# Layer norm's order, panels of the second block on VectorE, and the first norms inside the query projection

## The chip, the core and the metric

The program runs on one core of one Trainium2 chip. The metric is the device time of one execution in microseconds (us): the median of three runs of the kernel before is 1155.9 us (1153.77 to 1156.81).

The engines are named as the profile names them: PE (TensorE matmul), PEld (its weight loads), DVE (VectorE), ACT (ScalarE), POOL (GpSimd) and SP (SyncE, which here only issues the weight DMAs).

## What is computed

The reference is a two-block transformer forward in float32, with 256 tokens, width 1024 and one batch. The first block's parts, in order:

```python
# layer 0: x = x + conformer_conv(rms_norm(x))
u = h @ w_pw1 + b_pw1                          # 1024 -> 2048
a, gate = jnp.split(u, 2, axis=-1)
u = a * jax.nn.sigmoid(gate)                   # the gated linear unit ("glu")
u = depthwise_conv31(u, w_dw) + b_dw
u = jax.nn.silu(layer_norm(u, ln_g, ln_b))
x = x + u @ w_pw2 + b_pw2
# each layer then: x = x + memory_cross_attention(rms_norm(x), mem)
#                  x = x + swiglu(rms_norm(x))
# layer 1 has differential attention in place of the conv; rms_norm(x) at the end
```

The second block (`hybrid_layer`) projects the normed result once into queries, keys, values and gates, and attends in two families of eight heads each: a sliding window of 128 with sinks (the "w" heads), and a family with three branches (compressed, selected, window; the "n" heads). Its end is an output projection, and a feed-forward with a short causal conv.

```python
proj = rms_norm(h, attn_pre_norm) @ w_in        # q_n, k_c, v_c, k_s, v_s, k_w, v_w, g_n, q_w, k_sw, v_sw
ckv = compress(stack([rope(k_c), v_c]))         # windows of 32 tokens, stride 16 -> gelu MLP
o_swa = banded_attention(rope(q_w), rope(k_sw), v_sw, 128, sinks)
o_nsa = g0 * compressed + g1 * selected + g2 * banded(512)
h = h + rms_norm(concat(rms_norm(o_nsa), rms_norm(o_swa)) @ w_out)
```

## The kernel before

All projections are matmuls of a weight panel with activations. To keep float32 accuracy each operand is split into a rounded high part and the rest, and each product takes three matmuls: high by high, high by the activations' rest, and the panel's rest by high (line 409, in `gemm`). A panel is 128x1024 (512, 640 or 816 columns in some places). SP loads it into one of six stage buffers, ACT copies it to the high part `whi` (L276), and either DVE or POOL subtracts to get the low part `wlo` (L278). Which of the two does so is a cyclic string of letters for each weight in the table `LO`: `v` is DVE, `g` is POOL. The two parts stand in a ring of five buffers. Each time that `gemm` takes a panel (`consume`), it prepares panels up to `state["ahead"]`, five, beyond the one that it takes.

`gemm(K, xs, banks, evac, hooks)` runs K steps over the accumulator banks in PSUM (`acc`, six of them; two more are `aux`), calls the functions in `hooks` after the named step, and evacuates each bank at the end. The instructions of all engines are then ordered by a scheduler with priorities that follow the order in the source: a hook's place in the source decides roughly, not exactly, where its instructions stand in each engine's queue. Each engine's queue runs strictly in order.

RMS norms use the class `Stats`: squares on ACT, their sum `sacc` on POOL (L338; DVE for some), a fold of two halves `sfold` (L355), sums over partitions by PE with a column of ones (L361), a scale and offset on DVE (`ms`, L370), the power -1/2 on POOL (`rr`, L372), and where a row of factors is wanted over all partitions, `spread` on PE (L378). Layer norm after the conv has functions of its own: `ln_sum`, `ln_mean` (means by PE, subtraction, squares `lsq`, adds on DVE, L626) and `ln_rstd` (sums by PE, L632), which hang as hooks in the gemm of the memory's second value projection.

The places that the change touches:

- The glu after the first conv projection (L547 to L556), whose DVE operations scale the bank into an SBUF tile `t2`, then multiply.
- The layer norm's hooks (L622 to L645).
- The product `gfp` of two gain vectors (L959).
- The second block's start: `gemm(8, S0, BA, ...)` with the hook `norms` (L1000 on: two RMS norms chained, one through the other), then the first query projection `qw0`, whose hooks are `tables2` (spread and rotary tables `cR`, `sR`) and the evacuations `evA` of keys.
- The second block's attention, whose order is the list `ATT_SEQ`: `qw0`, `qw1`, `qn0`, `qn1` are query projections, `vt` values and gates, `xr` transposes of x, `ws` the window split (`winf`, `win`, on POOL and ACT, L1095 to L1097), `compk` and `compv` the compression MLPs, `a`, `b`, `c` with a number the scores, softmax and product with values of one head pair, `wo0` and `wo1` halves of the output projection. Scores are masked on DVE (L324), which also gives their maximum, and exponentiated on ACT (L1182 for the w heads).

## Time and profile before

| what | us |
|---|---|
| median of 3 runs | 1155.9 (1153.77 to 1156.81) |
| the profiled execution | 1154.35 |
| its span, first to last instruction | 1152.5 |
| PE busy | 1107.7 (96%) |
| DVE busy | 782.6 (68%) |
| ACT busy | 658.0 (57%) |
| POOL busy | 403.2 (35%) |

The profile is one execution. Times within it are counted from the span's start. PE's clock as granted by the chip is given as a share of full speed: 1.00 is 2.4 GHz, 0.50 is 1.2 GHz. A figure in square brackets behind a row is how long the engine sat idle before it, and what ended that idle time.

### The profile page before, as it was taken

The page shows a single profiled execution, that of the slowest core. Times are in us where ns is not written, and L with a number is a line of the kernel's source. Part 1 is how long each engine was busy: PE and PEld are TensorE (multiplying, and loading weights), DVE is VectorE, ACT ScalarE, POOL GpSimd, SP SyncE. Part 2 cuts the span into 40 slices and gives each one's busy share as a digit, 9 for nine tenths or more (in the row PEclk, how much of TensorE's full clock was granted, in tenths as well). Part 3 has the DMA queues.
Part 4 walks back from the last instruction along what each step waited for, and adds up shares of the span by engine and source line. Part 5 has one row for each costly group of instructions (what it writes and reads, how often), then busy time and mean ns, then how long its engine had stood idle before and what let it go on. Part 6 is the DMA issues. An engine that isn't in the chain of part 4 may idle for free.

```text
span 1152.5 us, 21545 instructions
## 1 busy us (share of the span) xinstructions
PE 1107.7 (96%) x8418; PEld 1048.2 (91%) x8418; DVE 782.6 (68%) x1432; ACT 658.0 (57%) x1165; POOL 403.2 (35%) x268
## 2 busy tenths in 40 slices
PE   7999989999999999999999999999988998999997
PEld 6898878999999999999899999999886678999986
DVE  6899867676676458766745655746678746887843
ACT  6555476665555345676756554536575745765632
POOL 5999947130000005731726443002662300112300
PEclk9999989999999999999999999999898998999999
DMA  7576535346545645544334654754563015464651
GB/s 248 191 256 208 195 110 182 124 140 211 189 150 200 215 152 166 196 133 129 128 127 158 197 182 144 253 173 137 181 200 130 19 56 182 152 205 161 226 191 37
DMA packets 59799, 191.13 MB, mean 166 GB/s; under 512 B 6752, under 2 KB 10080, under 8 KB 59696
## 3 DMA queue, kind: packets, MB, share of 16 engines
q1 hardware_dynamic: 58288, 187.31, 49.1%
q0 software_dynamic: 688, 1.90, 0.6%
q8 instruction: 66, 1.08, 0.4%
q10 hardware_dynamic: 720, 0.53, 0.1%
q14 instruction: 37, 0.30, 0.1%
HBM read 188.15 MB, written 1.05 MB: 164 GB/s over the span
## 4 chain that ended last, share of the span: by engine, by line
PE 46%; ACT 2%; DVE 2%; issue 2%; POOL 1%; POOLq 0%; DVEq 0%; ACTq 0%
PE acc L409 38%; PE acc L1125 1%; PE acc L1223 1%; ACT whi L276 1%; PE acc L696 1%; PE acc L730 0%; POOL sacc L338 0%; PE acc L1284 0%; PE acc L1288 0%; DVE wlo L278 0%; PE aux L1265 0%; PE acc L1377 0%; DVE memK1l L587 0%; PE acc L1285 0%; PE acc L1220 0%
## 5 line engine op out<-in xcount | busy, mean ns | idle before, releaser
L276 ACT ACTIVATE whi<-wf 128x1024 fp32r<-128x1024 f32 (+3 forms) x382 | 371.4, 987 | 301.4 <-PE acc L409 264.8
L278 DVE TENSOR_TENSOR wlo<-wf,whi 128x1024 fp32r<-128x1024 f32 (+2 forms) x261 | 327.8, 1264 | 183.7 <-ACT whi L276 178.3
L409 PE MATMUL acc<-s0h,whi 128*128 128x256 f32 x1192 | 338.5, 284 | 6.2 <-ACT whi L276 5.4
L409 PE MATMUL acc<-s0h,wlo 128*128 128x256 f32 x1192 | 335.5, 282 | 4.0 <-POOL wlo L278 3.6
L409 PE MATMUL acc<-s0l,whi 128*128 128x256 f32 x1192 | 335.7, 282 | 1.7 <-DVE s0l L437 1.7
L278 POOL TENSOR_TENSOR wlo<-wf,whi 128x1024 fp32r<-128x1024 f32 (+1 forms) x121 | 261.8, 2186 | 164.7 <-ACT whi L276 162.6
L409 PEld LDWEIGHTS acc<-s0h,whi 128*128 128x128 f32 x1192 | 226.7, 190 | 7.2 <-ACT whi L276 5.4
L409 PEld LDWEIGHTS acc<-s0h,wlo 128*128 128x128 f32 x1192 | 226.5, 190 | 5.7 <-POOL wlo L278 5.0
L409 PEld LDWEIGHTS acc<-s0l,whi 128*128 128x128 f32 x1192 | 226.9, 190 | 2.9 <-DVE s0l L437 2.1
L409 PE MATMUL acc<-s1h,whi 128*128 128x256 f32 x736 | 206.1, 281 | 0.7 <-ACT s1h L651 0.7
L409 PE MATMUL acc<-s1h,wlo 128*128 128x256 f32 x736 | 205.4, 279 | 0.7 <-DVE pad L665 0.4
L409 PE MATMUL acc<-s1l,whi 128*128 128x256 f32 x736 | 205.5, 280 | 0.0
L409 PEld LDWEIGHTS acc<-s1h,whi 128*128 128x128 f32 x736 | 138.3, 188 | 1.7 <-ACT s1h L651 1.4
L409 PEld LDWEIGHTS acc<-s1h,wlo 128*128 128x128 f32 x736 | 138.4, 188 | 1.1 <-DVE pad L665 0.7
L409 PEld LDWEIGHTS acc<-s1l,whi 128*128 128x128 f32 x736 | 138.6, 188 | 0.3 <-DVE pad L785 0.2
L409 PE MATMUL acc<-hh,whi 128*128 128x256 f32 x352 | 98.3, 279 | 0.0
L409 PE MATMUL acc<-hl,whi 128*128 128x256 f32 x352 | 98.3, 279 | 0.0
L409 PE MATMUL acc<-hh,wlo 128*128 128x256 f32 x352 | 98.3, 279 | 0.0
L338 POOL TENSOR_TENSOR sacc<-sq,sacc 128x512 f32<-128x512 f32 x21 | 33.3, 1588 | 124.0 <-ACT sq L337 123.7
L545 DVE SCALAR_TENSOR_TENSOR aux<-u,vecs,aux 128x256 f32<-128x256 f32 x174 | 68.6, 480 | 1.2 <-ACT aux L543 1.2
L409 PEld LDWEIGHTS acc<-hh,whi 128*128 128x128 f32 x352 | 66.2, 188 | 0.0
L409 PEld LDWEIGHTS acc<-hh,wlo 128*128 128x128 f32 x352 | 66.2, 188 | 0.0
(372 smaller groups left out, 1713.5 us busy)
## 6 DMA issues: line engine op xcount, KB each, us to landing
wf<-in_gu SPq DMA_DIRECT2D x120, 512.0 KB, 3.8
wf<-in_w_down SPq DMA_DIRECT2D x66, 512.0 KB, 4.3
wf<-in_mem_w_k SPq DMA_DIRECT2D x16, 512.0 KB, 4.0
wf<-in_mem_w_v SPq DMA_DIRECT2D x16, 512.0 KB, 3.5
wf<-in_mem_w_q SPq DMA_DIRECT2D x16, 512.0 KB, 3.5
wf<-in_mem_w_o SPq DMA_DIRECT2D x16, 512.0 KB, 3.7
wf<-in_w_pw SPq DMA_DIRECT2D x24, 256.0 KB, 3.0
wf<-in_gv SPq DMA_DIRECT2D x24, 256.0 KB, 2.6
```

What stands on the lines that cost most here:

```text
L276: p["ih"] = SC.activation(p["hi"][:, :W], p["f"][:, :W], AF.Copy)
L278: p["il"] = eng.tensor_tensor(p["lo"][:, :W], p["f"][:, :W], p["hi"][:, :W].bitcast(F32), op=OP.subtract)
L338: self.ins = self.eng.tensor_tensor(self.acc, sq, self.acc, op=OP.add)
L409: PE.matmul(o, l, r, start=(ki == 0 and n == 0 and q == 0), stop=(ki == K - 1 and q == 2), skip_group_check=True)
L545: V.scalar_tensor_tensor(cv[:, c] if k == TAPS - 1 else ai, src, w, ai, op0=OP.mult, op1=OP.add)
L696: PE.matmul(s[:, t * S:(t + 1) * S], l[:, c, t * 128:(t + 1) * 128], r[:, 2 * h + c], start=(t == 0 and c == 0 and n == 0), stop=(c == 1), ...
L1125: PE.matmul(ph[0:60, 0:256], win[:, a, 4 * g + j], w[:, j * 256:(j + 1) * 256], start=(g == 0 and j == 0 and w is p["hi"]), stop=(g == 3 a ...
L1223: PE.matmul(f, q1, kk[:, kv], start=True, stop=True, skip_group_check=True)
```

## The change

Seven edits are made together:

1. The glu multiplies in place in PSUM; the SBUF tile `t2` is gone.
2. `ln_mean` runs after step 3 (was 4), `ln_rstd` after step 6 (was 5). Of the three adds of squares on DVE two are left; the last group of squares goes through four more small matmuls instead. The spread factor is read from PSUM directly (`raw=True`), without ACT's copy.
3. `gfp` is issued after `st.ins`, which is a POOL instruction.
4. `norms` leaves the gemm `BA` (after its step 6) and goes into the gemm `qw0` (after its step 1); `tables2` and the key evacuations go from step 2 of `qw0` to its step 6.
5. In `LO`, `mq1` (second layer's memory query) goes from one panel in three on POOL to none; `T` (values, second block), `cmp` (compression) and `w` (output projection) go from one, two and one letter on POOL to none. Three panels of `mq1` and nine of the second block (one `T`, six `cmp`, two `w`) so move from POOL to DVE.
6. `ATT_SEQ` gets `few` after `qn0`: from there `ahead` is 1.
7. It also gets eight steps `p1` to `p5`: `pn` prepares panels up to n beyond those taken.

```diff
--- before.py
+++ after.py
@@ -62,10 +62,10 @@
 
 DIFF_SEQ = """q0 q1 a0 a1 V0 b0 a2 b1 a3 c0 q2 b2 c1 V1 b3 c2 a4 f0 c3 a5 q3 f1 b4 b5""".split()
 DIFF_END = {0: "a6 c4", 1: "a7 c5 b6", 2: "c6", (3, 1): "f2 b7", (4, 0): "c7", (5, 1): "f3"}
-ATT_SEQ = """... compk a4 qn0 compv c2 a5 b4 a6 comp2 c3 b5 c4 comp3 ... c7 a9 a10 b9 b10 a11 a12 c8 b11 c9 c10 a13 b12 c11 sw a14 a15 b13 c12 b14 wo0 c13 b15 wo1 c14 c15""".split()
+ATT_SEQ = """... compk a4 qn0 few compv c2 a5 b4 p1 a6 comp2 c3 b5 p2 c4 comp3 ... c7 a9 p1 a10 b9 p2 b10 a11 p3 a12 c8 b11 p4 c9 c10 a13 b12 p5 c11 sw a14 a15 b13 c12 b14 wo0 c13 b15 p4 wo1 c14 p4 c15""".split()
 LO = dict(pw1s="gv", pw1="g", mk="g", mv="g", pw2="gggvvvvv", mq="gggvvvvv", mo="vgv", gu0="v", gv0="v",
-          dn0="v", K="v", q="g", V="g", o="v", mq1="gvv", mo1="vgv", gu1="gv", gv1="v",
-          dn1="v", A="v", T="vvg", cmp="ggv", B="v", w="gv", W="v", gu2="v", gv2="vgv", dn2="v")
+          dn0="v", K="v", q="g", V="g", o="v", mq1="v", mo1="vgv", gu1="gv", gv1="v",
+          dn1="v", A="v", T="v", cmp="v", B="v", w="v", W="v", gu2="v", gv2="vgv", dn2="v")
 
 
 def _constants():
@@ -547,12 +547,10 @@
     def glu(c0):
         def f(j, ps):
             c = c0 + j
-            if 1:
-                t = poolC.tile([128, 2, S], F32, name="t2", tag="t2")
-                V.tensor_tensor(t, b2(ps), two(Rb[0]), op=OP.mult)
-                sg = poolC.tile([128, S], F32, name="sg", tag="sg")
-                SC.activation(sg, t[:, 1], AF.Sigmoid, bias=vc("b_pw1", 8 + c))
-                V.scalar_tensor_tensor(u[:, c, TAPS - 1:], t[:, 0], vc("b_pw1", c), sg, op0=OP.add, op1=OP.mult)
+            V.tensor_tensor(b2(ps), b2(ps), two(Rb[0]), op=OP.mult)
+            sg = poolC.tile([128, S], F32, name="sg", tag="sg")
+            SC.activation(sg, ps[:, S:2 * S], AF.Sigmoid, bias=vc("b_pw1", 8 + c))
+            V.scalar_tensor_tensor(u[:, c, TAPS - 1:], ps[:, 0:S], vc("b_pw1", c), sg, op0=OP.add, op1=OP.mult)
         return f
 
     def norm0():
@@ -622,15 +620,16 @@
             V.tensor_tensor(cp, cp, two(mu[:, :S]), op=OP.subtract)
             LN[j] = tmp.tile([128, 2, S], F32, name="lsq", tag="sq" if j else "sacc")
             SC.activation(LN[j], cp, AF.Square)
-            if j:
+            if 0 < j < 3:
                 V.tensor_tensor(LN[0], LN[0], LN[j], op=OP.add)
 
     def ln_rstd():
         ss = aux()
-        for i in range(2):
-            for t in range(2):
-                PE.matmul(ss[:, t:t + 1], LN[0][:, i, t * 128:(t + 1) * 128], ones[:, 0:1],
-                          start=(i + t == 0), stop=(i == 1), skip_group_check=True)
+        for j in (0, 3):
+            for i in range(2):
+                for t in range(2):
+                    PE.matmul(ss[:, t:t + 1], LN[j][:, i, t * 128:(t + 1) * 128], ones[:, 0:1],
+                              start=(j + i + t == 0), stop=(j == 3 and i == 1), skip_group_check=True)
         scr = small.tile([128, 2], F32, name="scr", tag="scr")
         SC.activation(scr[:, 0:1], LN[3][:, 0, 0:1], AF.Silu)
         LN["st"] = st = Stats(eps=1e-5)
@@ -639,10 +638,10 @@
     gemm(8, mT, FM8, mem_k(0))
     gemm(8, mT, TM4, mem_v(0))
     gemm(8, mT, FM8, mem_k(1))
-    gemm(8, mT, TM4, mem_v(1), hooks={2: [ln_sum], 4: [ln_mean], 5: [ln_rstd]})
+    gemm(8, mT, TM4, mem_v(1), hooks={2: [ln_sum], 3: [ln_mean], 6: [ln_rstd]})
     st = LN["st"]
     with tc.high_priority():
-        rs = spread(st.r)
+        rs = spread(st.r, raw=True)
         for s in (slice(0, 1), slice(1, 2), slice(2, 4), slice(4, 6), slice(6, 8)):
             cp = cv[:, s]
             V.tensor_tensor(cp, cp, rs[:, None, :].to_broadcast([128, s.stop - s.start, S]), op=OP.mult)
@@ -956,7 +955,8 @@
 
     sa, sb = Stats(), Stats()
     gfp = const.tile([128, 8], F32, name="gfp")
-    V.tensor_tensor(gfp, vecs[:, VOFF["g_final"][0]:VOFF["g_final"][0] + 8], vecs[:, VOFF["g_pre"][0]:VOFF["g_pre"][0] + 8], op=OP.mult)
+    with tc.issue_after(st.ins.ins):
+        V.tensor_tensor(gfp, vecs[:, VOFF["g_final"][0]:VOFF["g_final"][0] + 8], vecs[:, VOFF["g_pre"][0]:VOFF["g_pre"][0] + 8], op=OP.mult)
 
     def last(j, ps):
         xp = x[:, 2 * j:2 * j + 2]
@@ -1107,8 +1107,8 @@
 
     V.memset(kc2[64:128, :, :, S - 1:S], 0.0)
     pA = []
-    gemm(8, S0, BA, lambda j, ps: pA.append(ps), hooks={6: [norms]})
-    qw0_hooks = {2: [tables2] + [lambda j=j: evA(j, pA[j]) for j in range(3)]}
+    gemm(8, S0, BA, lambda j, ps: pA.append(ps))
+    qw0_hooks = {1: [norms], 6: [tables2] + [lambda j=j: evA(j, pA[j]) for j in range(3)]}
 
     kcmp = P1.tile([128, 2, 32], F32, name="kcmp")
     vcmp = P1.tile([32, 2, 64], F32, name="vcmp")
@@ -1306,7 +1306,9 @@
     steps = dict(xr=x2_rows, ws=window_split, vt=lambda: gemm(8, S0, [[("T", t, 0, 408)] for t in range(2)], evT),
                  qw0=lambda: q_(qw, 0, qw0_hooks), qw1=lambda: q_(qw, 1), qn0=lambda: q_(qn, 0), qn1=lambda: q_(qn, 1),
                  compk=lambda: comp(0), compv=lambda: comp(1), comp2=comp2, comp3=comp3, sw=sw.finish,
-                 wo0=lambda: wo1(0), wo1=lambda: wo1(1))
+                 wo0=lambda: wo1(0), wo1=lambda: wo1(1), few=lambda: state.update(ahead=1))
+
+    steps.update({f"p{n}": (lambda n=n: prep_to(state["use"] + n)) for n in range(1, 6)})
     for w in ATT_SEQ:
         if w in steps:
             steps[w]()
```

What the scheduler makes of it is seen in three places of the engines' orders. In them `wlo<-wf,whi` is a panel's subtraction, and the line numbers of the two kernels differ by up to two.

The first place is DVE around the second block's first norms: from the first norm's `ms` (L370) to the rotary tables (L1019, L1020). Before:

```order
L278 TENSOR_TENSOR wlo<-wf,whi 128x816
L370 TENSOR_SCALAR ms<-aux 128x2
L1008 TENSOR_TENSOR ms<-aux,rr 128x2
L278 TENSOR_TENSOR wlo<-wf,whi 128x816
L1009 TENSOR_TENSOR ms<-ms,rr 128x2
L1010 TENSOR_SCALAR ms<-ms 128x2
L1009 TENSOR_TENSOR ms<-ms,rr 128x2
L1010 TENSOR_SCALAR ms<-ms 128x2
L1019 TENSOR_TENSOR cR<-cst,aux 128x256
```

After:

```order
L278 TENSOR_TENSOR wlo<-wf,whi 128x816 x3
L370 TENSOR_SCALAR ms<-aux 128x2
L1008 TENSOR_TENSOR ms<-aux,rr 128x2
L1009 TENSOR_TENSOR ms<-ms,rr 128x2
L1010 TENSOR_SCALAR ms<-ms 128x2
L1009 TENSOR_TENSOR ms<-ms,rr 128x2
L1010 TENSOR_SCALAR ms<-ms 128x2
L278 TENSOR_TENSOR wlo<-wf,whi 128x816
L1019 TENSOR_TENSOR cR<-cst,aux 128x256
```

The panel subtraction that stood inside the chain of small operations now stands behind it. On PE the two sums of these norms (L361) stand 27 matmuls of `gemm` later than before, and the spread (L378) 24 later.

The second place is POOL from the key windows' DMAs to the first softmax operation of the n heads (L1253). `kc` are the shifted keys, `gp` is a gain row. Before:

```order
L1084 DMA kc_9653<-kcv 64x255
L278 TENSOR_TENSOR wlo<-wf,whi 128x1024 x3
L1095 TENSOR_TENSOR winf<-kc_9653,vecs 128x16x15 x2
L1097 TENSOR_TENSOR win<-winf,win 128x16x30
L1095 TENSOR_TENSOR winf<-kc_9653,vecs 128x16x15 x2
L1321 DMA gp_11139<-in_g_post 128x1024
L1097 TENSOR_TENSOR win<-winf,win 128x16x30
L278 TENSOR_TENSOR wlo<-wf,whi 128x1024 x5
L1253 TENSOR_SCALAR p<-p,dsm 128x128 x2
```

After:

```order
L1084 DMA kc_9646<-kcv 64x255
L1095 TENSOR_TENSOR winf<-kc_9646,vecs 128x16x15 x2
L1097 TENSOR_TENSOR win<-winf,win 128x16x30
L1095 TENSOR_TENSOR winf<-kc_9646,vecs 128x16x15 x2
L1323 DMA gp_11132<-in_g_post 128x1024
L1097 TENSOR_TENSOR win<-winf,win 128x16x30
L1253 TENSOR_SCALAR p<-p,dsm 128x128 x2
```

All eight panels have left; the window sums follow the DMAs at once.

The third place is DVE at the last masked scores (L324) ahead of the first n-head queries. Before:

```order
L278 TENSOR_TENSOR wlo<-wf,whi 128x1024
L324 ISA acc,mx<-acc,cst,nsink 128x128
L324 ISA mx 128x1
L324 ISA acc,mx<-acc,cst,nsink 128x256
L324 ISA mx 128x1
L278 TENSOR_TENSOR wlo<-wf,whi 128x1024
L1188 TENSOR_TENSOR dsm<-dsm 128x2
```

After:

```order
L278 TENSOR_TENSOR wlo<-wf,whi 128x1024 x3
L324 ISA acc,mx<-acc,cst,nsink 128x128
L324 ISA mx 128x1
L278 TENSOR_TENSOR wlo<-wf,whi 128x1024
L324 ISA acc,mx<-acc,cst,nsink 128x256
L324 ISA mx 128x1
L278 TENSOR_TENSOR wlo<-wf,whi 128x1024
L1188 TENSOR_TENSOR dsm<-dsm 128x2
```

Five panels stand there in place of two. At the rotation of the queries (`qn`, L1036) that follows, DVE has one panel ahead of the last step and two behind it, then masked scores again, in both kernels. From `cR` to those scores DVE's queue holds 15 panels, where it held 10.

DVE's queue begins alike in both: `gfp` (L959 and its counterpart) stands directly ahead of the first fold `sfold` (L355) before and after.

## Rows read from the trace of the kernel before

**Rows 1.** Busy time of the engines, from the page

```profile
PE 1107.7 (96%) x8418; PEld 1048.2 (91%) x8418; DVE 782.6 (68%) x1432; ACT 658.0 (57%) x1165; POOL 403.2 (35%) x268
```

**Rows 2.** PE's waits: line, engine waited for; us in all, times, longest

```profile
PE aux L361 <- POOL sfold L355: 4.7, 4, 2.5
...
PE acc L1223 <- ACT sp L1182: 3.6, 1, 3.6
PE acc L1125 <- POOL win L1097: 3.4, 1, 3.4
PE acc L696 <- DVE ql L591: 2.3, 1, 2.3
...
PE aux L361 <- DVE sfold L355: 1.1, 1, 1.1
```

**Rows 3.** PE's four waits and what follows: stretch, length, engines' busy time, PEclk, DMA

```profile
560.94:563.22 2.28, 0.01 (x1) 0.01 (x1) 2.28 (x4) 2.28 (x4) 1.07 (x1) 0.96 0.16 16
563.22:566.46 3.24, 3.24 (x15) 3.24 (x16) 2.64 (x4) 1.14 (x3) 3.15 (x3) 0.50 0.72 236
811.27:813.74 2.47, 0.00 (x2) 0.00 (x1) 1.90 (x2) 0.00 (x0) 2.39 (x3) 0.69 0.85 262
813.74:819.05 5.31, 5.31 (x25) 5.31 (x26) 1.68 (x6) 0.88 (x1) 2.27 (x3) 0.50 0.81 255
847.01:850.40 3.39, 0.00 (x2) 0.00 (x1) 1.26 (x3) 1.02 (x3) 2.62 (x3) 0.91 0.90 286
850.40:853.18 2.78, 2.78 (x13) 2.78 (x14) 0.00 (x0) 1.34 (x2) 2.44 (x4) 0.50 0.07 28
871.77:875.37 3.60, 0.00 (x0) 0.00 (x0) 3.60 (x13) 0.96 (x5) 0.00 (x0) 0.76 0.78 270
875.37:880.49 5.12, 5.12 (x18) 4.08 (x19) 2.51 (x16) 3.07 (x14) 0.00 (x0) 0.50 0.47 190
```

**Rows 4.** Matmuls of 256 columns (L409) alone, at either clock

```profile
814.60:819.00 4.40, 4.39 (x20) 0.50 0.76 224
820.50:823.80 3.30, 3.30 (x28) 1.00 0.50 159
```

**Rows 5.** DVE before the second memory attention: start, duration, engine, line, op, count

```profile
556.23 6.33 DVE L587 TENSOR_TENSOR memK1l<-memK,memK1h 128x512 fp32r<-128x512 f32 x4 [1.13 <-ACT memK1h L585]
```

**Rows 6.** POOL in the same stretch

```profile
559.27 2.74 POOL L278 TENSOR_TENSOR wlo<-wf,whi 128x1024 fp32r<-128x1024 f32 x1
```

**Rows 7.** DVE, the rotary tables

```profile
820.74 0.42 DVE L1019 TENSOR_TENSOR cR<-cst,aux 128x256 f32<-128x256 f32 x1 [3.32 <-PE aux L378]
```

**Rows 8.** From the rotary tables to the masked scores: all engines

```profile
820.74:873.29 52.55, 47.08 (x331) 43.26 (x329) 42.47 (x90) 36.03 (x72) 30.97 (x23) 0.97 0.56 181
```

**Rows 9.** The same stretch, panel subtractions (L278) alone: DVE, POOL

```profile
820.74:873.29 52.55, 18.44 (x10) 20.29 (x8) 0.97 0.56 181
```

**Rows 10.** DVE alone with a panel, and beside POOL

```profile
830.21 1.21 DVE L278 TENSOR_TENSOR wlo<-wf,whi 128x1024 fp32r<-128x1024 f32 x1
...
857.15 3.47 DVE L278 TENSOR_TENSOR wlo<-wf,whi 128x1024 fp32r<-128x1024 f32 x1
860.55 2.36 DVE L1188 TENSOR_TENSOR dsm<-dsm 128x2 f32<-128x2 f32 x1
...
868.84 4.53 DVE L278 TENSOR_TENSOR wlo<-wf,whi 128x1024 fp32r<-128x1024 f32 x2
873.29 0.35 DVE L324 CUSTOM_DVE_ANT_0 acc<-acc,cst,nsink 128x128 f32<-128x128 f32 x1
```

**Rows 11.** POOL, window sums

```profile
846.15 2.36 POOL L1095 TENSOR_TENSOR winf<-kc,vecs 128x240 f32<-128x240 f32 x2
849.23 1.11 POOL L1097 TENSOR_TENSOR win<-winf,win 128x480 fp32r<-128x480 f32 x1 [0.72 <-ACT win L1096]
```

**Rows 12.** DVE before the first norm

```profile
15.05 1.17 DVE L959 TENSOR_TENSOR gfp<-vecs 128x8 f32<-128x8 f32 x1
```

**Rows 13.** PE, layer norm's sums

```profile
151.99 1.05 PE L632 MATMUL aux<-ones,lsq 128*128 128x1 f32 x8 [1.76 <-DVE lsq L626]
```

## What is predicted

> **What bounds the kernel now.** I began with the engines' busy time: PE is busy for 1107.7 of 1152.5 us, so 44.8 us of the span are all that better order can win, less the slow stretches of PE's clock [rows 1]. Then the waits of PE, by line: the reader is to see that a few single waits of 2 to 4 us make up much of it, and that four of them lie where the change works [rows 2]: `ql` of the second memory attention (2.3), the folds `sfold` (4.7 over four, the longest 2.5), the window sums `win` (3.4) and the masked and exponentiated scores `sp` (3.6). Third, the stretches of these four waits and of what follows each [rows 3]: while PE waits, DVE or POOL is at work, and right after each wait PE's granted clock is 0.50, which is 1.2 GHz in place of 2.4. The stretches at half clock last 3.24, 5.31, 2.78 and 5.12 us, together 16.45.
>
> What half clock costs is read from one kind of matmul: 20 take 4.40 us at 0.50 (0.220 us each) and 28 take 3.30 us at 1.00 (0.118 each) [rows 4]. So 0.46 of each microsecond at half clock is lost: 1.5, 2.4, 1.3 and 2.4 us, in all 7.6. The Trainium skill, "TensorE: Matmul & The Clock Gate", section on HAM oscillation, reckons the penalty of a throttled period as half of it, which would make 8.2 us of the same 16.45. The trace is a little below that rule, and I go by the trace.
>
> **Second memory attention (`mq1` on VectorE).** Four subtractions `memK1l` take 6.33 us on DVE [rows 5], and the last of them runs beside POOL's panel of 2.74 us [rows 6]; `ql`, for which PE waits 2.28 us, is queued behind it. That POOL panel goes. What can be won is the wait and the half clock behind it, 2.28 + 1.5 = 3.8 us. Three panels come to DVE at 1.21 us each; two of them stand behind `ql`, and the `ms` and power chain of the next norm is queued close to them. I take 3.0 us. From below: one panel ahead of `ql` would put 1.21 back and leave the clock low, a gain of 1.1; with two more ahead of what PE needs next, a loss of 1.3.
>
> **The second block's first norms.** The sums stand 27 matmuls later, 27 x 0.118 = 3.2 us, so PE, which began to wait for the second at 811.27 [rows 3], comes to it at about 814.2 (its wait of 0.3 us for the first is gone too), and POOL had folded it by 813.74; PE's wait of 2.47 us and 2.4 us of half clock go, 4.9 together. The spread stands 24 matmuls later (2.8 us), so PE comes to it 4.9 - 2.8 = 2.1 us earlier than before, and with 0.3 us of the first sum's shorter wait 2.4 us earlier. The panel that stood in the chain of small operations is behind it now, so I expect the chain to be ready by then. `cR`, which began at 820.74 [rows 7], begins at about 818.4. PE's gain of 4.9 is thus only lent: DVE, which rotates everything, gains 2.4.
>
> **The attention: who is late next.** From here to the masked scores behind `qn`, 52.55 us, PE is busy 47.08 us, DVE 42.47 and POOL 30.97 [rows 8]; of DVE's time 18.44 are ten panels, and POOL spends 20.29 on eight [rows 9]. Without its four losses (2.47 + 2.4 + 3.39 + 1.3) and the 3.60 us at the end, PE would reach L1223 13.2 us earlier, at 862.2 in place of 875.37.
>
> DVE can't follow so far. A panel takes 1.21 us there alone; beside POOL's panels one took 3.47, an operation on two elements per partition took 2.36, and the two panels ahead of the masked scores took 4.53 [rows 10]. With POOL's panels gone, DVE's other work is 42.47 - 18.44 = 24.0 us, less about 2.2 for that small operation, 21.8. The queue now holds 15 panels, 15 x 1.21 = 18.2. Together 40.0 us from 818.4: 858.4 if DVE never waits. Before, it stood idle for 52.55 - 42.47 = 10.1 us; if it does so again, 868.5. Half of that idle time I expect to go, since part of it was PE's own waiting, which makes 863.4. POOL still runs the window sums, now right after the DMAs, where four panels stand in DVE's queue. Two `winf` took 2.36 and `win` 1.11 us before [rows 11], and there are two such sets. I charge 1 us for the collision and have the masked scores start at 864.4, in place of 873.29 [rows 10]: about 9.0 us gained, with bounds of 4.8 (all the idle time stays) and 14.9 (none). The half clock behind it I leave as it is, as PE, due at 862.2, still waits there.
>
> On that collision there is a rule: the Trainium skill, "GPSIMD Engine Reference", key points, says that GpSimd shares its SBUF interfaces with VectorE and that they contend when the VectorE instruction has two SBUF inputs, as a panel's subtraction has. By it the panels that stand beside the window sums would stretch as those beside POOL's panels did; with three at 3.47 - 1.21 = 2.26 the charge is 6.8 us, and the sum of this part 3.2 in place of 9.0. The trace has a panel on DVE at its undisturbed 1.21 us and others at up to 3.47, so it shows the rule at work, but not always at DVE's expense.
>
> `few` and `p1` to `p5` change when later panels are prepared. The stage buffers still load six panels ahead, and each panel that is left gets a step of its own before it is used; I cost it at nothing, hidden behind PE's matmuls on the panel before. If that cover is gone, a panel late by its subtraction costs 1.21 us, and there are six (two of `qn1`, four of `wo0` and `wo1`), 7.3 in all.
>
> **The rest.** `gfp` takes 1.17 us ahead of the first `sfold` [rows 12], for which PE waits 1.1 us [rows 2]. It stands at the same place in DVE's queue as before, directly ahead of that fold, so that this part of the change doesn't do what it says: gain 0, and 1.1 if the chip shows otherwise. In the layer norm an add on DVE goes and the sums double: PE waited 1.76 us for the last add, and the sums took 1.05 us [rows 13]. At best 1.8 is won, at worst 1.05 lost; I take 0.5, since the last of the two adds that are left is the slow one. The glu in PSUM shortens DVE's work in a stretch of which no wait of over a microsecond is named in [rows 2]; PE's projections of the memory cover it. Gain 0.3, with bounds of 1 us to either side: the banks are held longer, and if PE comes to one too early it waits.
>
> **Sum.** 3.0 + 9.0 + 0.5 + 0.3 = 12.8 us, from the profiled execution's 1154.35: 1141.5. That execution was 1.55 us below the median of the runs, and what I forecast is a median: 1143. By the bounds, the gains reach from -1.3 + 4.8 - 1.05 - 1 = 1.5 to 3.8 + 14.9 + 1.8 + 1 + 1.1 = 22.6, with late panels taking up to 7.3 more off.
>
> **Rivals.** First, DVE's load eats most of it: the idle time stays (4.8 gained there) and the collision costs some 2 us, with 1.1 from `mq1` and nothing else; 3.9 to 8 us in all, 1148 to 1152.4. For it speaks that DVE is nearly as long as PE in that stretch after the change (40.0 against about 44); against it, that no panel of POOL's is left to slow DVE. Chance 0.14.
>
> Second, slower: DVE becomes the bound of the attention. Five panels stand around the last masked scores in place of two, and PE's banks come free only after these. With the idle time kept (868.5) and each of five panels stretched by 2.26, the scores start at 879.8, 6.5 us later than before, which with nothing won elsewhere makes 1155.9 + 6.5 = 1162. It decides from 4.8 / 2.26, that is from the third stretched panel on. Against it: the stretched ones in the trace all ran beside POOL's panels [rows 10], which are gone. Chance 0.07.
>
> Third, that the change gives a microsecond here and there and loses it again: late panels after `few` (7.3) and a kept idle time against 9.0 and 3.0. Time about 1155, within 0.3%. Chance 0.11.
>
> Fourth, it does better: PE meets all four places in time and DVE's idle time goes, and with it the half clock after L1223 (2.4 more); 12.8 + 5.9 + 2.4 = 21, to 1135. Chance 0.06.
>
> The forecast itself, 1137 to 1148, has 0.62. About 0.3%, 3.5 us, is what a measurement can tell from no change. Faster by more than that: 0.62 + 0.14 + 0.06 = 0.82; within: 0.11; slower: 0.07. The range that leaves out 0.2 at most: 1135 to 1153.
>
> **What would show it.** In the profile after: PE's waits for `ql`, `sfold` (2.5) and `win` gone from the list, and the clock at 1.00 after them; `gfp` still ahead of `sfold`, with PE's 1.1 us wait there; no panel on DVE of much over 1.3 us after the window sums; the masked scores behind `qn` at some 860 to 868; a wait of PE at L1223 that is shorter, yet there. Wrong would make it: PE waits on `wlo` in `qn1` or the output projection, panels of over 2 us on DVE without POOL's beside them, or a new wait on `kss` or `qw` right after `cR`.

## The result and the profile after

The changed kernel takes 1141.37 us (median of 4 runs, 1139.79 to 1141.62); the kernel before took 1154.89 in the same session (4 runs, 1153.77 to 1156.81). The ratio of after to before is 0.9877, with a 95% interval of 0.9864 to 0.9890: 1.1 to 1.4% less, 14.2 us of 1155 by the ratio and 13.5 by the medians. The profiled execution of after took 1141.31 us with a span of 1139.1, so 13.4 us less span than the profiled execution of before.

Busy time of the engines, from the page of after (it answers [rows 1]): PE is busy 4.1 us less, POOL 31.

```profile
PE 1103.6 (97%) x8426; PEld 1044.7 (92%) x8426; DVE 779.3 (68%) x1443; ACT 656.5 (58%) x1164; POOL 372.1 (33%) x256
```

PE's waits in after (line, engine waited for; us in total, times, longest), against [rows 2]: `ql` and L1223's `sp` are gone from the list, the long `sfold` too (the longest left is 1.5), `win` is halved, a wait on `p` (the memory attention's exponentials) at L718 is new, and one on `spT` (the w heads' transposed exponentials) has grown from 0.3 us to 1.2. The first `sfold` of DVE is as it was.

```profile
PE aux L361 <- POOL sfold L355: 3.1, 4, 1.5
PE acc L1125 <- POOL win L1097: 1.7, 1, 1.7
PE aux L718 <- ACT p L712: 1.5, 1, 1.5
...
PE acc L1206 <- ACT spT L1196: 1.2, 1, 1.2
...
PE aux L361 <- DVE sfold L355: 1.1, 1, 1.1
```

The stretches of after that answer to [rows 3] (stretch, length; busy time of PE, PEld, DVE, ACT, POOL; PEclk, DMA). In their order: the new wait for `p`; the stretch behind the sums of the second block's first norms, at full clock up to the tables; the stretch from `cR` to the masked scores [rows 8]; the wait for `win`; L1223, where PE is busy from the start at 1.00; and the two stretches at half clock, the one behind the wait for `p` and the one that begins within the wait for `win`.

```profile
564.70:566.25 1.55, 0.03 (x1) 0.00 (x1) 0.19 (x2) 1.25 (x6) 1.55 (x2) 1.00 0.56 225
...
811.00:815.30 4.30, 4.30 (x39) 4.30 (x39) 2.60 (x9) 1.32 (x2) 1.41 (x2) 1.00 0.77 296
814.35:858.54 44.19, 40.94 (x285) 38.02 (x283) 41.38 (x96) 33.83 (x69) 12.69 (x15) 0.96 0.61 192
838.70:840.45 1.75, 0.02 (x1) 0.00 (x0) 1.75 (x5) 0.51 (x2) 1.16 (x2) 0.83 0.75 260
...
862.04:867.16 5.12, 5.12 (x40) 4.30 (x41) 4.41 (x26) 4.12 (x19) 0.00 (x0) 1.00 0.04 18
566.79:570.20 3.41, 3.41 (x17) 3.41 (x17) 3.08 (x5) 2.28 (x6) 0.90 (x1) 0.50 0.42 138
839.86:843.27 3.41, 2.82 (x13) 2.82 (x14) 3.06 (x5) 0.43 (x1) 3.11 (x4) 0.50 0.32 99
```

Panel subtractions alone in the stretch from `cR` to the masked scores (DVE, POOL), against [rows 9]: fifteen on DVE take hardly longer than ten did, and POOL has none. (The sixteenth that the row counts is the last 0.08 us of one that began at 813.42.)

```profile
814.35:858.54 44.19, 18.90 (x16) 0.00 (x0) 0.96 0.61 192
```

DVE in after, instruction by instruction (start, duration, engine, line, operation, count). They answer to [rows 12], [rows 5], [rows 7] and [rows 10]. The panels ahead of the masked scores take 1.18 us each in place of 2.26, and one group of three, at 824.50, is stretched by 0.9.

```profile
14.60 1.17 DVE L959 TENSOR_TENSOR gfp<-vecs 128x8 f32<-128x8 f32 x1
...
551.46 4.15 DVE L585 TENSOR_TENSOR memK1l<-memK,memK1h 128x512 fp32r<-128x512 f32 x4 [1.13 <-ACT memK1h L583]
555.54 0.68 DVE L589 TENSOR_TENSOR ql<-acc,qh 128x512 fp32r<-128x512 f32 x1
...
559.37 1.28 DVE L686 TENSOR_SCALAR kap<-rr 128x2 f32<-128x2 f32 x1 [0.22 <-POOL rr L372]
...
562.89 1.26 DVE L699 SCALAR_TENSOR_TENSOR mx<-mx,kap 128x2 f32<-128x2 f32 x1
...
814.35 0.41 DVE L1019 TENSOR_TENSOR cR<-cst,aux 128x256 f32<-128x256 f32 x1
...
824.50 4.55 DVE L278 TENSOR_TENSOR wlo<-wf,whi 128x1024 fp32r<-128x1024 f32 x3
...
839.45 0.97 DVE L1188 TENSOR_TENSOR dsm<-dsm 128x2 f32<-128x2 f32 x1
...
845.08 3.50 DVE L278 TENSOR_TENSOR wlo<-wf,whi 128x1024 fp32r<-128x1024 f32 x3 [2.12 <-ACT whi L276]
...
856.28 2.35 DVE L278 TENSOR_TENSOR wlo<-wf,whi 128x1024 fp32r<-128x1024 f32 x2
858.54 0.35 DVE L324 CUSTOM_DVE_ANT_0 acc<-acc,cst,nsink 128x128 f32<-128x128 f32 x1
```

POOL in after, the window sums [rows 11]. The first `win` waits 11.33 us for ScalarE's copy (L1096), which begins at 838.62, behind three panels and all eight of ScalarE's exponentials of the first heads.

```profile
824.68 3.28 POOL L1095 TENSOR_TENSOR winf<-kc,vecs 128x240 f32<-128x240 f32 x2 [3.07 <-DVE qw L1036]
839.29 1.11 POOL L1097 TENSOR_TENSOR win<-winf,win 128x480 fp32r<-128x480 f32 x1 [11.33 <-ACT win L1096]
```

PE in after: the layer norm's sums and the spread behind them [rows 13].

```profile
149.88 1.95 PE L631 MATMUL aux<-ones,lsq 128*128 128x1 f32 x16 [1.43 <-DVE lsq L624]
...
152.88 0.71 PE L378 MATMUL aux<-cst,rr 128*128 128x128 f32 x4 [0.48 <-POOL rr L372]
```

Laid side by side, the starts of the same instruction on PE in the two traces give the ledger of the gain (us):

| PE's instruction | before | after | gain so far |
|---|---|---|---|
| a transpose ahead of the second layer's memory attention | 539.11 | 534.35 | 4.8 |
| first scores of that attention's last head group (L695) | 571.56 | 563.15 | 8.4 |
| a matmul of the gemm behind it (L409) | 574.94 | 570.04 | 4.9 |
| a transpose of x, behind the tables (L1105) | 824.81 | 815.11 | 9.7 |
| first matmul on `win` (L1125) | 850.40 | 840.45 | 9.95 |
| first n-head scores (L1223) | 875.37 | 862.04 | 13.3 |
| compression MLP, behind before's half clock (L1163) | 881.53 | 865.91 | 15.6 |
| output projection (L409) | 918.89 | 905.06 | 13.8 |
| end of the span | 1152.5 | 1139.1 | 13.4 |

### The profile page after: what moved, and what is told of

Its sections match the earlier page's. It is cut to its first block, busy times and chain, and to the rows that moved or that the text cites. A ratio compares the mean times of both kernels' runs of the same rounds, so it can differ in the third digit from the quotient of the medians.

```text
span 1139.1 us, 21550 instructions
## 1 busy us (share of the span) xinstructions
PE 1103.6 (97%) x8426; PEld 1044.7 (92%) x8426; DVE 779.3 (68%) x1443; ACT 656.5 (58%) x1164; POOL 372.1 (33%) x256
## 3 DMA queue, kind: packets, MB, share of 16 engines
q8 instruction: 66, 1.08, 0.4%
HBM read 188.15 MB, written 1.05 MB: 166 GB/s over the span
## 4 chain that ended last, share of the span: by engine, by line
PE 44%; issue 2%; DVE 2%; POOL 1%; ACT 1%; POOLq 0%; DVEq 0%; ACTq 0%
PE acc L409 38%; PE acc L1125 1%; PE acc L729 0%; PE acc L1223 0%; DVE wlo L278 0%; PE aux L1265 0%; PE acc L1284 0%; PE acc L1288 0%; PE acc L1379 0%; POOL kc L1084 0%; POOL winf L1095 0%; DVE acc L324 0%; PE acc L1285 0%; PE acc L1206 0%; PE acc L695 0%
## 5 line engine op out<-in xcount | busy, mean ns | idle before, releaser
L278 DVE TENSOR_TENSOR wlo<-wf,whi 128x1024 fp32r<-128x1024 f32 (+3 forms) x273 | 337.2, 1245 | 184.4 <-ACT whi L276 179.0
L409 PE MATMUL acc<-s0h,whi 128*128 128x256 f32 x1192 | 336.7, 283 | 6.4 <-ACT whi L276 5.5
L409 PE MATMUL acc<-s0h,wlo 128*128 128x256 f32 x1192 | 334.4, 281 | 3.3 <-POOL wlo L278 3.2
L409 PE MATMUL acc<-s0l,whi 128*128 128x256 f32 x1192 | 334.6, 281 | 0.8 <-DVE s0l L437 0.8
L278 POOL TENSOR_TENSOR wlo<-wf,whi 128x1024 fp32r<-128x1024 f32 (+1 forms) x109 | 230.8, 2142 | 133.1 <-ACT whi L276 131.2
L409 PEld LDWEIGHTS acc<-s0h,whi 128*128 128x128 f32 x1192 | 225.6, 189 | 7.6 <-ACT whi L276 5.5
L409 PEld LDWEIGHTS acc<-s0h,wlo 128*128 128x128 f32 x1192 | 225.2, 189 | 4.9 <-POOL wlo L278 4.5
L409 PEld LDWEIGHTS acc<-s0l,whi 128*128 128x128 f32 x1192 | 225.5, 189 | 1.5 <-DVE s0l L437 1.2
L409 PE MATMUL acc<-s1h,whi 128*128 128x256 f32 x736 | 206.4, 281 | 0.0
L409 PE MATMUL acc<-s1l,whi 128*128 128x256 f32 x736 | 206.0, 280 | 0.0
L409 PE MATMUL acc<-s1h,wlo 128*128 128x256 f32 x736 | 205.6, 280 | 0.0
L409 PEld LDWEIGHTS acc<-s1h,whi 128*128 128x128 f32 x736 | 139.1, 189 | 0.4 <-ACT s1h L436 0.2
L409 PEld LDWEIGHTS acc<-s1l,whi 128*128 128x128 f32 x736 | 139.0, 189 | 0.3 <-DVE pad L784 0.2
L409 PEld LDWEIGHTS acc<-s1h,wlo 128*128 128x128 f32 x736 | 138.8, 189 | 0.0
L409 PE MATMUL acc<-hh,whi 128*128 128x256 f32 x352 | 98.3, 279 | 0.0
L409 PE MATMUL acc<-hl,whi 128*128 128x256 f32 x352 | 98.3, 279 | 0.0
L409 PE MATMUL acc<-hh,wlo 128*128 128x256 f32 x352 | 98.3, 279 | 0.0
L409 PEld LDWEIGHTS acc<-hl,whi 128*128 128x128 f32 x352 | 66.2, 188 | 0.0
L409 PEld LDWEIGHTS acc<-hh,wlo 128*128 128x128 f32 x352 | 66.2, 188 | 0.0
```

The source lines that it names most:

```text
L278: p["il"] = eng.tensor_tensor(p["lo"][:, :W], p["f"][:, :W], p["hi"][:, :W].bitcast(F32), op=OP.subtract)
L409: PE.matmul(o, l, r, start=(ki == 0 and n == 0 and q == 0), stop=(ki == K - 1 and q == 2), skip_group_check=True)
```

## The experiments

Gains are against the kernel before on the same chip: 1 less the ratio, times its time of about 1155 us.

**The panels of `mq1` alone.** Is the wait for `ql` worth 3 to 3.8 us?

```diff
-          mq1="gvv"
+          mq1="v"
```

> The kernel before with mq1's panels on VectorE alone. Theory A: the wait for ql (2.28) goes and comes back as a wait for p in front of the transposes (about 1.5), with half a clock stretch behind it, because the norm's ms now stands behind two panels; 0 to 0.5 us gained. Theory B, the prediction: 3.0 us gained and no new wait.

1151.94 us, ratio 0.9966 (0.9950 to 0.9982): 3.9 us, from 2.1 to 5.7. The interval holds the forecast 3.0. In the profile the wait for `ql` is gone, and a wait of 1.5 us for `p` (L713 there) stands behind it, as in after. Here no half clock follows it. In the profiled execution of after one did (566.79 to 570.20). The profiled execution here, 1149.58 us, is one of the faster of ten runs (1148.02 to 1154.18), and PE's wait at L1223, which the edit doesn't touch, is 2.3 us in it in place of 3.6: the size is read from the runs.

**Layer norm and glu.**

```diff
+ (glu in PSUM; ln_mean after step 3, ln_rstd after step 6, one add less, raw spread)
```

> The kernel before with the glu in PSUM and the layer norm's new order alone (edits 1 and 2). Theory A, the stages add up, each worth what the checkpoints of the two traces show: by the fifth hundred microseconds the changed kernel is 4.8 us ahead, all of it from these two, so this kernel gains 4.5 to 5 us. Theory B, the prediction's sum: 0.8 us, and the rest of those 4.8 is an effect of other edits on the scheduler. The wait for the last add of squares (1.76 before) at 1.4, the clock at half for 3.4 us in place of 6.8.

1152.24 us, 0.9977 (0.9966 to 0.9988): 2.7 us, where 0.8 was forecast for the two.

**The glu alone** (edit 1 of the list).

> The kernel before with the glu in PSUM alone. e1 (glu and layer norm) gained 0.9977 in time, about 2.7 us. Theory A: the glu is worth the checkpoints' 1.1 to 1.3 us by the first memory projection, since VectorE's last product has one SBUF source less and is not held by GpSimd's panels, and nothing later; ratio 0.999. Theory B, the prediction's term for the glu: 0.3 us or no difference.

1154.06 us, 0.9987 (0.9975 to 0.9999): 1.5 us, so some 1.2 are the layer norm's. The glu alone is not told from its forecast of 0.3 by its interval (0.1 to 2.9 us); the two together are told from 0.8 (1.4 to 3.9).

**The norms alone.**

```diff
-    gemm(8, S0, BA, ..., hooks={6: [norms]})
-    qw0_hooks = {2: [tables2] + ...}
+    gemm(8, S0, BA, ...)
+    qw0_hooks = {1: [norms], 6: [tables2] + ...}
```

> The kernel before with the norms moved into qw0 alone (edit 4). Theory A: 4.9 us, the wait of 2.47 and the half clock behind it, kept to the end. Theory B, the prediction's word that it is only lent: GpSimd's panels ahead of the window sums take it back there, 2.4 us or less is left, and the wait for win grows from 3.4 towards 6.

1152.20 us, 0.9976 (0.9964 to 0.9989): 2.8 us, less than the 4.9 of PE. POOL and PE in its trace show why: a panel of the values' weight (`T`, 816 columns) stands on POOL between the sum and the fold, PE waits 2.60 us for that fold, as long as before, and 3.41 us at half clock follow.

```profile
809.71 2.28 POOL L338 TENSOR_TENSOR sacc<-sq,sacc 128x512 f32<-128x512 f32 x1
812.10 2.53 POOL L278 TENSOR_TENSOR wlo<-wf,whi 128x816 fp32r<-128x816 f32 x1
814.59 1.48 POOL L355 TENSOR_TENSOR sfold<-sacc 128x256 f32<-128x256 f32 x1
```

**The second block's panels and order alone** (letters of `T`, `cmp`, `w`; `few`, `p1` to `p5`).

> The kernel before with the second block's panels on VectorE and the new ATT_SEQ (edits 5 without mq1, 6 and 7), the norms where they were. Theory A, the stages add up: 3.5 to 4.5 us, what the changed kernel gains between the first scores and the end. Theory B, norms and attention need each other, as VectorE's chain starts later without the earlier norms: under 2 us or a loss. Theory C, each removes the same late window sums: 6 us or more alone.

1152.34 us, 0.9972 (0.9962 to 0.9981): 3.2 us. The wait at L1223 is gone, that for `win` (3.3) stays.

**The letters alone**, without `few` and `p1` to `p5`.

> The kernel before with T, cmp and w on VectorE and nothing else: ATT_SEQ and the norms as before. Theory A: the letters are what counts and few and p1 to p5 are worth nothing, so it gains what e3 gained, about 3.2 us. Theory B: without few the panels are prepared five ahead and stand in VectorE's queue in front of the scores; it gains less than 1 us or loses.

1150.35 us, 0.9958 (0.9943 to 0.9973): 4.9 us, 1.6 more than with them; the intervals overlap.

**Norms, letters and order together.**

> The kernel before with the norms in qw0 and the second block's panels on VectorE with the new ATT_SEQ: e3 and e4 together, which gained 3.2 and 2.8 us alone. Theory A, they add: 6.0 us. Theory B, each alone leaves the other's wait in its way (with the norms alone GpSimd's panels still hold the window sums; with the panels alone VectorE's chain still begins late), so together they gain 8 to 9 us, as the prediction's 9.0 and the checkpoints' 8.6 have it.

1145.47 us, 0.9920 (0.9904 to 0.9936): 9.2 us, which is the 9.0 of the prediction and 3.2 more than the two alone (2.8 + 3.2 = 6.0). The panel between sum and fold is one that the letter of `T` moves: on POOL no panel stands there now, PE's wait for that fold is 0.9 us in place of 2.6, none follows for the spread, and the clock stays at 1.00. That is 1.7 us of wait and, at a loss of 0.46, 1.6 of half clock: 3.3 us, as much as the two give more together. It may not be all of it, since the wait for `win` is shorter too (1.7 us; 3.2 and 3.3 with either alone).

```profile
810.01 2.28 POOL L338 TENSOR_TENSOR sacc<-sq,sacc 128x512 f32<-128x512 f32 x1
813.39 1.26 POOL L355 TENSOR_TENSOR sfold<-sacc 128x256 f32<-128x256 f32 x1 [1.10 <-PE aux L361]
```

**After, without `few` and `p1` to `p5`** (`ATT_SEQ` of before).

> The changed kernel with the ATT_SEQ of before: without few and p1 to p5 (edits 6 and 7 undone). e6, the letters without these edits, gained 0.9958, e3 with them 0.9972. Theory A, the steps cost something: 1 to 2 us gained by leaving them out. Theory B, they pay only with the norms moved and no panel left on GpSimd: 1 us or more lost. Theory C: no difference, and e3 and e6 differ by the spread of their runs.

1137.89 us, 0.9857 (0.9842 to 0.9872), 3.5 us below after by the medians and 2.3 by the ratios, whose intervals overlap. In the n heads' stretch PE is busy throughout; in after it is not (stretch, length, PE, PEld, DVE, ACT, POOL, PEclk, DMA). First after, then this kernel:

```profile
880.00:890.00 10.00, 8.72 (x43) 4.78 (x42) 8.39 (x53) 8.60 (x43) 2.54 (x6) 1.00 0.04 5
```

```profile
880.00:890.00 10.00, 10.00 (x53) 5.70 (x51) 7.73 (x43) 8.03 (x39) 3.87 (x10) 1.00 0.16 54
...
566.00:570.00 4.00, 3.22 (x26) 3.04 (x27) 2.54 (x7) 2.83 (x5) 2.15 (x1) 1.00 0.24 70
```

Its second line is the place behind the wait for `p`, here at full clock. By the starts of the same instructions, 1.8 of the 3.0 us between the two spans come from the n heads and 1.5 from that place; 0.5 go the other way at the layer norm, where this execution is at half clock for 6.83 us and that of after for 3.41.

The n heads' 1.8 us come with `few` and `p1` to `p5` in every trace. From the last matmul of the compression MLP (L1163) to the first of the output projection PE takes 36.7 us in each of the seven kernels without them, before among them, and 38.5 to 38.8 in each of the six with them; those six alone have waits of PE there, 0.8 to 1.4 us in all. (The kernel without them further down that runs at half clock in this stretch is left out.)

**The window sums earlier** (after, with `ws` behind `a1`).

```diff
-ATT_SEQ = """qw0 xr vt a0 a1 b0 a2 a3 qw1 ws c0 ...
+ATT_SEQ = """qw0 xr vt a0 a1 ws b0 a2 a3 qw1 c0 ...
```

> The changed kernel with the window split ws ahead of the first softmax (behind a1 in ATT_SEQ) in place of behind qw1. In the changed kernel win waits 11.3 us for ScalarE's copy, which stands behind eight exponentials and three panels in its queue, and TensorE then 1.7 us for win with half a clock stretch behind. Theory A, ScalarE's order holds win: the wait and the half clock go, 2 to 3 us gained on the changed kernel, about 1138.5. Theory B, the wait moves to the panels or the scores behind it, as so often here: no difference.

1144.15 us, 0.9907 (0.9890 to 0.9924): slower than after by 2.8 us. The wait for `win` goes, but ScalarE's copies now stand ahead of the gates' exponential and wait for POOL (first fence, ScalarE), and PE waits 4.30 us for that (second fence, PE).

```profile
830.22 0.61 ACT L1096 ACTIVATE win<-winf 128x480 fp32r<-128x480 f32 x1 [3.87 <-POOL winf L1095]
```

```profile
832.92 0.39 PE L409 MATMUL acc<-s0h,whi 128*128 128x256 f32 x1 [4.30 <-ACT gts L1065]
```

**The first window sum earlier, ScalarE's copy of it behind the gates.**

```diff
-ATT_SEQ = """qw0 xr vt a0 a1 b0 ...
+ATT_SEQ = """qw0 xr vt a0 a1 ws0 b0 ...
...
+            with ExitStack() as late:
+                if a == 0:
+                    late.enter_context(tc.issue_after(gate_op[0].ins))
+                SC.activation(win[:, a, :, 0:30], wf, AF.Copy)
```

> The changed kernel with the first window's copy on ScalarE behind the gates' exponentials, neither in front of them (e7, where ScalarE blocked on winf for TensorE's loss of 4.3 us) nor behind eight score exponentials. Theory A: win is ready by 832, TensorE's wait of 1.7 for it and the half clock behind go, and nothing waits for the copy; 2 to 3 us gained. Theory B: the stage is bound by the first softmax on VectorE, and TensorE waits as long for spT or the panels; under 0.5 us.

1138.07 us, 0.9856 (0.9839 to 0.9872): 3.3 us below after by the medians and 2.4 by the ratios, whose intervals overlap. ScalarE's copy stands at 826.93 in place of 838.62, and PE waits for `win` no more.

```profile
826.93 0.62 ACT L1102 ACTIVATE win<-winf 128x480 fp32r<-128x480 f32 x1
```

**`gfp` truly moved, and fewer panels ahead of the second memory attention.**

```diff
-    with tc.issue_after(st.ins.ins):
+    with tc.issue_after(lam_op[0].ins):    # lam_op: a DVE operation further back in the queue
+                if i and h == 1:
+                    state["ahead"] = 3
```

> The changed kernel with two more edits, far from each other so that the profile tells them apart: gfp issued behind a VectorE instruction of the first memory attention, so that it truly leaves the place ahead of the first sfold; and in the second memory attention panels prepared three ahead until the norm's ms is issued, so that ms stands ahead of the two panels. Theory A: TensorE's wait of 1.05 at 16 us goes; ms starts 2 us earlier after ql, and the wait of 1.5 for p and the half clock behind it go, 2 to 3 us; together 3 to 4 us on the changed kernel, about 1138. Theory B: gfp's microsecond is given back at the next power (rr), and p still comes late, as kap and mx run beside GpSimd's memV1l at 1.3 us each; under 1 us.

1141.41 us, 0.9888 (0.9873 to 0.9902): no change against after. `gfp` is gone from ahead of the first fold, but the fold, 0.41 us in after, takes 1.39 beside POOL's panels, so that PE waits 0.71 us in place of 1.05 (first line). The wait for `p` stays at 1.5, though the panels did move: `kap` takes 0.17 us in place of 1.28, and the exponentials begin 1.3 us earlier against the end of PE's wait than in after. But DVE's reciprocal of their sums (`sm`) stands in its queue behind a memset that waits 2.24 us for POOL's `memV1l`.

```profile
14.43 1.39 DVE L355 TENSOR_TENSOR sfold<-sacc 128x256 f32<-128x256 f32 x1
...
566.58 0.17 DVE L1155 MEMSET hv<- 128x128 f32 x1 [2.24 <-POOL memV1l L586]
566.67 0.11 DVE L710 RECIPROCAL sm<-sm 128x2 f32<-128x2 f32 x1
```

**Both edits that helped** (without `few` and `p1` to `p5`, first window sum earlier).

> The changed kernel with both of the edits that helped it alone: without `few` and `p1` to `p5` (1137.89 us alone, 3.5 below the changed kernel's 1141.37), and with the first of the two window sums issued behind the first two scores, ScalarE's copy of it behind the gates' exponential (1138.07 alone, 3.3 below). Theory A: the two losses are apart in time (the window sums' wait near 840 us and its half clock, the n heads' waits at 890 to 901 us), so the gains add: 3.5 + 3.3 = 6.8 us, about 1134.6, ratio 0.982 to 0.984, and no wait of PE of over 0.5 us from 830 to 935 us but those for `spT`. Rival B: what PE wins at the window sums it gives back at the next thing that is late, which sets the n heads' start in either kernel; then the two overlap and the time stays at 1137 to 1138.5, ratio 0.985 to 0.986.

1141.16 us (1140.18 to 1144.42), 0.9892 (0.9876 to 0.9909). Both theories fail: it is no faster than after, and 3 us slower than either edit alone. PE reaches the w heads' scores 6.5 us earlier than without the window edit (849.72 in place of 856.21), and DVE is late there. Three panels stand ahead of the masked scores (first fence, DVE), PE waits 1.68 and 1.00 us (second, PE), and then runs at half clock for 10.24 us (third, stretch).

```profile
849.46 3.48 DVE L278 TENSOR_TENSOR wlo<-wf,whi 128x1024 fp32r<-128x1024 f32 x3
852.86 0.35 DVE L324 CUSTOM_DVE_ANT_0 acc<-acc,cst,nsink 128x128 f32<-128x128 f32 x1
```

```profile
854.77 0.61 PE L1200 MATMUL aux<-cst,sp 128*128 128x128 f32 x3 [1.68 <-DVE sp L1197]
856.38 1.12 PE L1212 MATMUL acc<-spT,vall 128*64 128x256 f32 x2 [1.00 <-ACT spT L1202]
```

```profile
855.52:865.76 10.24, 9.38 (x35) 6.79 (x35) 5.43 (x26) 3.80 (x14) 0.00 (x0) 0.50 0.35 122
```

The kernel with `few` and the earlier window sum (1138.07 us) has one panel at that place, waits 1.46 us for `spT` alone, and runs at half clock for 3.41 us (DVE, then the stretch):

```profile
851.23 1.19 DVE L278 TENSOR_TENSOR wlo<-wf,whi 128x1024 fp32r<-128x1024 f32 x1
852.35 0.34 DVE L324 CUSTOM_DVE_ANT_0 acc<-acc,cst,nsink 128x128 f32<-128x128 f32 x1
```

```profile
856.93:860.34 3.41, 3.41 (x11) 2.52 (x10) 1.75 (x8) 1.12 (x6) 0.00 (x0) 0.50 0.42 132
```

So `few` has a use after all: it keeps panels out of DVE's queue ahead of these scores, which pays where PE comes early, against its cost in the n heads. Of the 3.8 us between these two spans (1139.3 and 1135.5) 3.3 are lost from these scores to the output projection, where PE goes from 1.6 us ahead to 1.7 behind. The half clock and the waits are enough for that: PE's 6.0 us more of work at half clock (9.38 against 3.41) cost 2.7 at a loss of 0.46, and the waits are 1.2 longer (2.68 against 1.46). This is read from one execution of each; that the kernel with both edits is the slower one shows in the runs, whose intervals don't overlap. The two versions with medians below both kernels are those of 1137.89 and 1138.07 us.

## Why the prediction held

The time was forecast at 1143 and came at 1141.4. The gain that it worked out from the profiled execution, 12.8 us, stands against 13.4 between the spans. That the sum fits so closely is in part luck: the second block's terms hold (8.4 for 9.0), but in this execution the early edits give 4.0 us more than forecast and `mq1` 2.9 less, and both differences hang in part on stretches at half clock that other executions don't share. The terms, one by one:

- **The norms: 4.9 for PE, measured 4.8** (4.9 to 9.7 in the ledger). Of the 2.47 us wait for the second fold 0.9 is left, and the half clock behind it is gone. That this gain would be lent only was wrong: the spread comes in time, PE does not stop there again, and keeps it. It takes the moved letter of `T` as well; without it the panel between sum and fold keeps the wait at 2.60 (the norms alone), which the prediction didn't name. DVE's own gain at `cR` was put at 2.4. It is 820.74 - 814.35 = 6.4 less the 4.9 won before the norms, 1.5.
- **DVE behind `cR`: right.** In the time of before, that is with the 4.9 us won earlier put back, the masked scores start at 858.54 + 4.9 = 863.4; forecast were 864.4. The queue held 40.0 us of work by the sum; DVE was busy 41.38 of 44.19 us. Its idle time fell from 10.1 to 2.8, where half, 5.0, was charged: the lower idle time makes up for `cR`, 0.9 later than forecast, and for the busier queue. The collision with the window sums, 1 us, is the 4.55 for three panels, 0.9 above 3 x 1.21. A second one, `dsm` at 0.97 us beside `win`, comes ahead of an idle stretch of DVE of 2.12 us. The rival worked out there had three panels stretched by 6.8 us in all. The rule of the Trainium skill named beside it ("GPSIMD Engine Reference", key points) says that the two engines contend when the VectorE instruction has two SBUF inputs. The trace agrees, at a lower price and partly on POOL's side: the three panels took 4.55 us, where three without a neighbour took 3.50 (at 845.08), and the two `winf` beside them 3.28, against 2.36 in [rows 11].
- **L1223: wrong in its picture.** A shorter wait and half clock were to be left. There is neither [rows 3]: the wait for `win` and its half clock, thought gone, stayed (1.7 us and 3.41 at half clock), and a wait of 1.2 for `spT` came. PE so arrives at 862.04 + 4.9 = 866.9, behind the scores. Without the two waits and what that half clock costs, 1.7 + 1.2 + 1.3 (0.46 of the 2.82 us that PE works in it), it would have been 862.7; forecast was 862.2. The gain up to there is 13.3 - 4.9 = 8.4, against 9.0. The reason that `win` was late was missed: I looked at POOL's panels ahead of it, and ScalarE's copy, in the middle of the chain, was queued behind exponentials. The two window experiments, in which the copy stands earlier and the wait is gone, show that it is this copy.
- **After L1223: two terms that cancel.** The half clock that goes gives 2.3 more (13.3 to 15.6), and the n heads take 1.8 back (15.6 to 13.8). `few` and `p1` to `p5` were cost at nothing, with a loss of up to 7.3 from late panels. No panel was late. What they cost is those 1.8 us, which every trace with them shows and none without. The run times agree, though each time with intervals that overlap: the kernels without them are faster by 1.6 (before's norms) and 2.3 to 3.5 us (after). Why PE comes to wait in the n heads wasn't taken apart further.
- **`mq1`: 3.0 forecast, 3.9 alone, 0.1 in the profiled execution of after.** There 3.6 us are won up to 571.56, and 3.5 given back by the wait for `p` and by half clock. That wait was not forecast as such, only that the next chain stands close. It does not come from the panels that stand behind the first `ql`, nor from `kap` (1.28): in the kernel that moved both it stays. What is left in both traces is POOL's `memV1l`, with `mx` (1.26 and 1.27) beside it on DVE and, ahead of `sm`, a memset that waits for it. No run takes `memV1l` off POOL, so this stays an argument.
- **The early edits: 0.8 forecast, 2.7 measured alone, 4.8 in the profiled execution.** The layer norm's bounds held (`lsq` 1.76 to 1.43, sums 1.05 to 1.95), but the waits behind the sums were left out: PE's wait for `rr` falls from 1.38 to 0.48, and one of 0.69 behind the spread goes. Together that is 0.33 - 0.90 + 0.90 + 0.69 = 1.0 us, near the 1.2 of the runs, where 0.5 was forecast; the glu's 1.5 was put at 0.3. This is the mis-sized term. That the stretch at half clock falls from 6.83 us to 3.41 between these two executions is not the edit's doing: of the seven kernels with before's order four have 3.41 there, and of the seven with the new one three.
- **`gfp`: 0 forecast, 0 measured.** It stands where it stood, and PE waits its 1.1 us. Truly moved it gives 0.3.

What the slow rivals needed does not occur: DVE's idle time does not stay, and behind `cR` every panel takes some 1.2 us but those beside `winf`. The parts measured alone add up to 2.7 + 3.9 + 9.2 = 15.8 us, against 14.2 by the ratio of all: within their intervals.

## What to carry to other kernels

A chain that crosses three engines (here POOL, ScalarE, POOL) is late by its slowest queue: before blaming the first engine, look at what stands ahead of the middle one. A transfer of work between engines should be judged in the order that results: two edits worth 2.8 and 3.2 us were worth 9.2 together, for the most part because one cleared the queue that the other needed, and two with medians some 3 us lower each gained nothing together, where the trace shows PE coming early to a third engine that was late.

## What the hardware showed that was not expected

**The same wait is followed by different lengths of half clock.** Over the profiled executions of the fourteen kernels the 2.3 us wait for `ql` was followed by half clock in all seven that had it, the 1.5 us wait for `p` in one of seven (after). At the layer norm, the stretch at half clock lasted 3.41 us in seven kernels, 6.83 in six and, in the kernel with the glu alone, 10.23, and either order of the layer norm has both of the shorter ones:

```profile
151.77:162.00 10.23, 8.38 (x29) 6.52 (x28) 5.21 (x10) 6.81 (x15) 1.64 (x1) 0.50 0.17 58
```

At 0.46 us lost for each in which PE works, 3.41 us at half clock cost up to 1.6 us, more than some of the edits here, so that one profile alone can't size an edit to better than that.

**DVE and POOL exclude each other for whole instructions.** The two-element `dsm` of after, at 839.45, takes 0.97 us and ends at 840.42; POOL's `win` beside it runs from 839.29 to 840.40. In the layer norm and glu kernel, whose profiled execution is the slowest of its ten runs (1155.95 us), one DVE panel takes 5.82 us, to 186.27, beside the last two of three POOL panels and a sum that ends at 185.19 (DVE, then POOL):

```profile
180.45 5.82 DVE L278 TENSOR_TENSOR wlo<-wf,whi 128x1024 fp32r<-128x1024 f32 x1
```

```profile
176.87 7.10 POOL L278 TENSOR_TENSOR wlo<-wf,whi 128x1024 fp32r<-128x1024 f32 x3
183.94 1.25 POOL L338 TENSOR_TENSOR sacc<-sq,sacc 128x512 f32<-128x512 f32 x1
```

In after the same panel, beside the same three, takes 2.26, and POOL's three 8.09 us in place of 7.10:

```profile
180.84 2.26 DVE L278 TENSOR_TENSOR wlo<-wf,whi 128x1024 fp32r<-128x1024 f32 x1
```

The Trainium skill, "SBUF — State Buffer", section "SBUF: two separate sides", says that the port pair of the two engines is an exclusive lock, taken by a VectorE operation with two SBUF inputs or by one of GpSimd: who starts first has it for the whole instruction, and the other blocks fully. The traces agree: `dsm` ends 0.02 us behind `win`, and the panel of 5.82 us ends 1.08 behind POOL's sum, which is nearly the 1.21 that a panel takes alone. The 5.82 us show besides that DVE can lose several turns in a row: POOL went on to its next operation twice while the panel waited. PE's wait for the operation behind that panel is 4.33 us, where in after it is 0.76.
